# Pair order for the preparations of a seven-product matmul, and residual rows loaded five pairs later

## The chip, the cores and the metric

One core of a Trainium2 chip runs the kernel. Times are microseconds of device time. Three executions of the kernel before were timed; the metric is their median. One further execution was profiled.

## The reference, cut to what matters

One layer of a decoder trunk in float32, 512 tokens of width 2048. Two token mixers (a gated recurrence and a forgetting attention) are projected up, gated and added; the change does not touch them. It touches the two large products that end in a normalised residual:

```python
merged = sigmoid(g_a) * y_a + sigmoid(g_b) * y_b            # 512 x 2048
x = x + rms_norm(merged @ w_o, norm_mix_post)               # w_o: 2048 x 2048
h = rms_norm(x, norm_ffn_pre)
gate, up = split(h @ w_ffn_in, 2)                           # each 512 x 5632
x = x + rms_norm((silu(gate) * up) @ w_ffn_down, norm_ffn_post)   # w_ffn_down: 5632 x 2048
```

## The kernel before, in words

Every float32 operand is cut into a high part (a ScalarE copy to the matmul's fp32r type) and a low part (a VectorE subtraction), and each product is three matmuls: high by low, low by high, high by high. A weight tile of 128 x 1024 thus costs a load on SP's DMA queue into a raw buffer, a copy on ScalarE and a subtraction on VectorE, before TensorE can use it.

`merged @ w_o` and the down projection are done by the class `Rows` as block products of 2 x 2 blocks with seven multiplications in place of eight (p1 to p7). A *pair* is two row blocks of the weights, 2 x 128 rows of 2048 columns, held as four tiles a, b, c, d of 128 x 1024. The products need sums of these tiles, kept in a running tile `t` of the pair, and sums of the activations, written to DRAM beforehand (`md` for `w_o`, `actd` for the down projection; `token_parts`). Since eight PSUM banks hold only two products at a time, the work goes in stages, each of which passes over all pairs: W1 (p7, p6), W2 (p1, p5), W3 (p4), D0 and D1 (p2 and p3, one column half each) over 8 pairs of `w_o`; K1 (p7, p3), K2 (p1, p6), K3 (p5, p2), K4 (p4) over 22 pairs of the down projection. The items of a stage are numbered through: `wo0` to `wo7` are the pairs in W1, `wo8` is the first in W2, `wo24` the first in D0; `dn0` to `dn21` are K1, `dn22` to `dn43` K2, `dn44` to `dn65` K3, `dn66` to `dn87` K4.

For one item, `load` issues on SP's queue the loads of `t` (from the weights in the first stage; of five pairs of the down projection from a DRAM copy later), of the tiles that the stage needs and of the pair's activation sums x (line 749). `split` then issues the copies (lines 771 and 792 on ScalarE), the sums (lines 785 and 816 on VectorE) and the low parts (lines 775 and 825 on VectorE); where `t` lives in DRAM it is written back from SP's queue (line 829). `run` keeps the loads three items and the splits two items ahead of the matmuls in the order in which the program is traced.

That order isn't the order on the engines. The framework's scheduler places the instructions of each engine by readiness in its own timing model, ties going to the earlier traced one; an instruction whose inputs it believes to be there earlier is placed ahead. Once placed, an engine's instructions run strictly in that order, and each waits for its semaphores. `tc.issue_after(ins)` adds, for what its block traces on the same engine as `ins`, the condition that it is placed behind `ins`; nothing waits for `ins` to finish.

Buffers: three raw weight tiles (tag `wraw`, used for a, c, cd, and d in K1), three more (`wrawx`: d in the other stages, and tiles of `t` that live in DRAM), ten part buffers (`wpart`, a high and a low one for each tile in use, four for a pair with two products, two for one with a single product) which TensorE frees, and sixteen tiles of 128 x 1024 (`wide`) which hold most `t`, all x, the norm weights of the last stage and the residual rows.

At the end of a stage the banks are taken (`take`): copies on ScalarE (line 889) or sums on VectorE (lines 883 and 935). When a column block of the output is complete, `done` multiplies it with the norm weights (line 990 for `w_o`, line 1181 for the down projection), and `finish_rows` adds the residual (line 1175) and stores the rows. The residual rows for that are loaded by `x1_hook` in K4 (line 1163), eight loads of 512 KB, one in each of eight successive pairs.

Of the kernel before, what the change touches and what calls it, by code (L numbers as in the profile page):

```python
# [8 lines left out]
F32 = mybir.dt.float32  # L9
F32R = mybir.dt.float32r  # L10
U32 = mybir.dt.uint32
AF = mybir.ActivationFunctionType
ALU = mybir.AluOpType
# [30 lines left out]
def block_kernel(ctx: ExitStack, tc: tile.TileContext, x, w_in, b_fox_f, hgrn_lb_logits, hgrn_norm_w,  # L44
                 w_up_a, w_up_b, w_o, norm_mix_pre, norm_mix_post, norm_ffn_pre, norm_ffn_post,
                 w_ffn_in, w_ffn_down, out):
    nc = tc.nc
# [14 lines left out]
    def wide(name, dtype=F32, shape=(P, 1024)):  # L62
        return bigp.tile(list(shape), dtype, tag="wide", name=name, bufs=NX)
# [54 lines left out]
    loads = []  # L118
    state = {"i": 0}

    def wpart(name):
        return wp.tile([P, 1024], F32R, tag="wpart", name=name, bufs=NHALF)
# [49 lines left out]
    def split(src, name):  # L172

        hi = big(name + "h", F32R)
        lo = big(name + "l", F32R)
        nc.scalar.activation(hi, src, AF.Copy)
        nc.vector.tensor_tensor(lo, src, hi.bitcast(F32), ALU.subtract)
        return hi, lo
# [189 lines left out]
    def hgrn_head(h, r):  # L368
# [99 lines left out]
        for w in range(2):  # L468
            pw = paired(pot, w) if w == 0 else paired(pot, w)[:, :, ::-1]
            ow, gw = [a.rearrange("p (j w t) -> p j w t", w=2, t=P)[:, :, w, :] for a in (o, sg)]  # L470
            nc.vector.scalar_tensor_tensor(ow, pw, nw_f, gw, ALU.mult, ALU.mult)
        oa.append(split(o, n + "o"))
        yield

# [192 lines left out]
    class Rows:  # L667


        def __init__(self, name, w, parts, order, items, done, place_t):  # L670
            self.name, self.w, self.parts, self.order, self.items, self.done = name, w, parts, order, items, done
            self.place_t = place_t
            self.n_loaded = self.n_split = 0
            self.raw, self.ready, self.t, self.acc, self.x_kept, self.later = {}, {}, {}, {}, {}, []

# [9 lines left out]

        def load_to(self, n):
            while self.n_loaded < min(n, len(self.items)):
                self.load(self.n_loaded)
                self.n_loaded += 1

        def load(self, n):
            kind, i = self.items[n]
# [62 lines left out]
        def split_to(self, n):  # L755
            while self.n_split < min(n, len(self.items)):
                self.load_to(self.n_split + 1)
                self.split(self.n_split)
                self.n_split += 1

        def split(self, n):
            kind, i = self.items[n]
            nm = f"{self.name}{n}"
            got = self.raw.pop(n)
            tt = nc.vector.tensor_tensor

            def parts_of(src, tag):

                hi, lo = wpart(f"{nm}{tag}h"), wpart(f"{nm}{tag}l")
                for a, cs in src:  # L770
                    nc.scalar.activation(hi[:, cs], a, AF.Copy)

                def make_lo():
                    for a, cs in src:
                        tt(lo[:, cs], a, hi[:, cs].bitcast(F32), ALU.subtract)
                return hi, lo, make_lo

            def one(which):
                return [(got[which], slice(0, 1024))]

            def add_t(op, a, reverse=False, to=None):

                for u, cs in t:
                    o = u if to is None else to[:, cs]
                    tt(o, *((a[:, cs], u) if reverse else (u, a[:, cs])), op)

            t = one("t") if "t" in got else self.t.get(i)
            names = PRODUCTS[kind]
            width = 256 * len(names)
            xh, xl = got["x"][:, 0:width], got["x"][:, width : 2 * width]  # L790
            if kind != "D1":
                nc.scalar.activation(xh, xl.bitcast(F32), AF.Copy)
            w = {}
            if kind == "K1":
                w["p3"] = parts_of(one("d"), "d")
                add_t(ALU.subtract, got["d"], reverse=True)
                w["p7"] = parts_of(t, "t")
            elif kind == "K2":
                w["p1"] = parts_of(one("a"), "a")
                add_t(ALU.add, got["a"])  # L800
                w["p6"] = parts_of(t, "t")
            elif kind == "K3":
                w["p2"] = parts_of(one("c"), "c")
                add_t(ALU.subtract, got["d"], reverse=True, to=got["d"])
                w["p5"] = parts_of(one("d"), "d")
                if not self.late_c(i):
                    add_t(ALU.subtract, got["c"])
            elif kind in ("K4", "W3"):
                if "c" in got:
                    add_t(ALU.subtract, got["c"])  # L810
                w["p4"] = parts_of(t, "t")
            elif kind == "W1":
                add_t(ALU.subtract, got["d"], reverse=True, to=got["d"])
                w["p7"] = parts_of(one("d"), "d")
                for u, cs in t:
                    tt(u, got["a"][:, cs], got["d"][:, cs], ALU.add)
                w["p6"] = parts_of(t, "t")
            elif kind == "W2":
                w["p1"] = parts_of(one("a"), "a")
                add_t(ALU.subtract, got["d"], reverse=True, to=got["d"])  # L820
                w["p5"] = parts_of(one("d"), "d")
            else:
                w["cd"] = parts_of(one("cd"), "c")
            if kind != "D1":
                tt(xl, xl.bitcast(F32), xh.bitcast(F32), ALU.subtract)
            for v in w.values():
                v[2]()
            if "t" in got and kind in ("K1", "K2") or "t" in got and kind == "K3" and not self.late_c(i):
                nc.sync.dma_start(self.t[i], got["t"])
            if kind[0] == "D":  # L830
                q = int(kind[1])
                h, l, _ = w["cd"]
                wq = {("p2", q): (h[:, F], l[:, F]), ("p3", q): (h[:, L], l[:, L])}
            else:
                wq = {(p, q): (w[p][0][:, (F, L)[q]], w[p][1][:, (F, L)[q]]) for p in names for q in range(2)}
            self.ready[n] = (wq, {p: (xh[:, j * 256 : (j + 1) * 256], xl[:, j * 256 : (j + 1) * 256])
                                  for j, p in enumerate(names)})
# [262 lines left out]
    def parts_to(i):  # L1100
        while ahead["w"] < min(i, len(work)):
            n = ahead["w"]
            ahead["w"] += 1
            j, p, _ = work[n]
            key = key_of(n)
            load_to(n + 1)
            a, b, c, d = (raws.get(key + (x,)) for x in "abcd")
            if p == "p7":
                nc.vector.tensor_tensor(d, d, b, ALU.subtract)  # L1109
            elif p == "p5":  # L1110
                nc.vector.tensor_tensor(b, b, a, ALU.subtract)
            elif p == "p6":
                nc.vector.tensor_tensor(a, a, d, ALU.add)  # L1113
            elif p == "p4":
                nc.vector.tensor_tensor(c, a, c, ALU.subtract)
            src = {"p1": a, "p2": c, "p3": d, "p7": d, "p5": b, "p6": a, "p4": c}[p]
            wh = wpart(f"fh{n}")
            wl = wpart(f"fl{n}")
            nc.scalar.activation(wh, src, AF.Copy)  # L1119
            nc.vector.tensor_tensor(wl, src, wh.bitcast(F32), ALU.subtract)  # L1120
            wparts[n] = (wh, wl)
# [14 lines left out]
    def ffn_ahead():  # L1136
        load_to(4)
        parts_to(2)
# [17 lines left out]
                wfp.extend((r[:, 0:S], r[:, S : 2 * S]))  # L1156

    def x1_hook(at):
        if 1 <= at < 9:
            t, half = t_row((at - 1) // 2), (at - 1) % 2  # L1160
            with tc.issue_after(loads[-1].ins):
                r = wide(f"x1r{t}_{half}")
                nc.sync.dma_start(r, x1d[t * P : (t + 1) * P, half * 1024 : (half + 1) * 1024])
                x1r[t, 2 * half], x1r[t, 2 * half + 1] = r[:, 0:S], r[:, S : 2 * S]
        if at in (10, 12):
            finish_rows(2 + (at - 10) // 2)

    def t_row(t):
        return (t + 2) % 4
# [3 lines left out]
    def finish_rows(t):  # L1173
        for c in range(4):
            nc.vector.scalar_tensor_tensor(mw[t, c], mw[t, c], rinv[t], x1r[t, c], ALU.mult, ALU.add)
            nc.sync.dma_start(out[t * P : (t + 1) * P, c * S : (c + 1) * S], mw[t, c])
# [18 lines left out]
    gt, ut, tt, prod, open_bank, acts = {}, {}, {}, {}, {}, {}  # L1195
    for n, (j, p, place) in enumerate(work):
        load_to(n + LOAD_AHEAD)
        parts_to(n + AHEAD)
        for i in range(2 * (n - 4), 2 * (n - 3)):
# [3 lines left out]
        at = place.index(p)  # L1203
# [3 lines left out]
        for i in range(KH):  # L1207
            cs = slice(i * P, (i + 1) * P)
# [71 lines left out]
```

## Time and profile before

| what | value |
|---|---|
| median of three executions | 2837.89 us (2835.57 to 2845.24) |
| the profiled execution | 2837.45 us |
| its span, first to last instruction | 2835.7 us |
| TensorE busy | 2766.2 us |
| VectorE busy | 1931.0 us |
| ScalarE busy | 1170.1 us |
| mean granted TensorE clock, as a share of full | 0.993 |

The seven-product stages stand at 1292 to 1468 us (`w_o`) and at 2371 to 2824 us (down projection) of the span. A row of a timeline is: start, duration, engine and line, operation, written tile <- read tiles, shapes, count; behind it in brackets the idle time of the engine just before and what ended it. PE is TensorE, DVE VectorE, ACT ScalarE, POOL GpSimd; SPq is SP's queue, which only issues transfers. Tile names carry the item's number; `dh`, `dl` are the high and low part of tile d, `th`, `tl` of t; buffer numbers are left out, so `dnt` and `wot` are the t of any pair. In a table by stretch the columns are: from and to, its length, busy us and number of instructions of PE, PEld (weight loads of TensorE), DVE, ACT and POOL, mean granted clock, mean busy share of the DMA engines, GB/s.

### The profile page before, as it was taken

To read this page: it belongs to the slowest core of one execution; us is meant where nothing else is said; L and a number is where in the kernel's file an instruction comes from. 1 tells how busy PE (TensorE), PEld (TensorE's weight loads), DVE (VectorE), ACT (ScalarE), POOL (GpSimd) and SP (SyncE) were. 2 spreads that over 40 slices of the span, in tenths; PEclk is the share of its full clock that TensorE was granted. 3 is DMA by queue.
4 is the path that set the end of the run, shared out by engine and by line. 5 is a ranking of instruction groups with operands and counts; after the bars stand their busy time and mean duration, and the time that the engine had idled before them with its cause. 6 is when DMAs were issued, how large, how long until landed. Compare 5 with 4: busy or idle time off the path is not lost.

```text
span 2835.7 us, 40418 instructions
## 1 busy us (share of the span) xinstructions
PE 2766.2 (98%) x16024; PEld 2433.8 (86%) x16024; DVE 1931.0 (68%) x2750; ACT 1170.1 (41%) x1557; POOL 45.0 (2%) x75
## 2 busy tenths in 40 slices
PE   9999999999999999998999999999999999999997
PEld 7788888888888888887789999999999999877876
DVE  4776675333343433457879988888888888777888
ACT  4554544222232342224565444444444444444444
POOL 1000000000000000000000000000000000000001
PEclk9999999999999999999999999999999999999999
DMA  6323323333333333467774544444444448755875
GB/s 164 97 75 85 82 76 85 97 97 97 101 90 89 89 86 99 128 209 255 241 233 117 178 144 123 127 131 129 126 124 132 128 127 267 246 171 172 279 260 175
DMA packets 504799, 406.39 MB, mean 143 GB/s; under 512 B 16617, under 2 KB 444186, under 8 KB 504610
## 3 DMA queue, kind: packets, MB, share of 16 engines
q1 hardware_dynamic: 504610, 403.81, 47.6%
q8 instruction: 126, 2.06, 0.3%
q14 instruction: 63, 0.52, 0.1%
HBM read 359.95 MB, written 43.79 MB: 142 GB/s over the span
## 4 chain that ended last, share of the span: by engine, by line
PE 84%; DMA 6%; DVE 6%; issue 2%; ACT 2%; SPq 0%; POOL 0%; DVEq 0%; POOLq 0%; ACTq 0%
PE b L152 3%; PE b L154 3%; PE b L153 3%; PE p L152 3%; PE p L153 3%; PE p L154 3%; PE ga L152 2%; PE ga L153 2%; PE ga L154 2%; PE gb L152 2%; PE gb L153 2%; PE gb L154 2%; PE ya L152 1%; PE ya L154 1%; PE ya L153 1%
## 5 line engine op out<-in xcount | busy, mean ns | idle before, releaser
L136 ACT ACTIVATE wh<-wr 128x1024 fp32r<-128x1024 f32 (+1 forms) x214 | 223.0, 1043 | 642.4 <-PE b L153 147.0
L137 DVE TENSOR_TENSOR wl<-wr,wh 128x1024 fp32r<-128x1024 f32 (+1 forms) x214 | 257.9, 1205 | 232.7 <-ACT wh L136 232.6
L1119 ACT ACTIVATE fh<-fid 128x1024 fp32r<-128x1024 f32 x88 | 93.3, 1060 | 182.5 <-DVE fid L1109 119.1
L152 PE MATMUL p<-x,wh 128*128 128x512 f32 x416 | 165.2, 397 | 1.7 <-DVE rb L272 1.7
L154 PE MATMUL p<-x,wl 128*128 128x512 f32 x416 | 164.6, 396 | 0.0
L153 PE MATMUL p<-x,wh 128*128 128x512 f32 x416 | 163.5, 393 | 0.0
L152 PE MATMUL b<-x,wh 128*128 128x512 f32 x384 | 154.1, 401 | 0.0
L154 PE MATMUL b<-x,wl 128*128 128x512 f32 x384 | 150.2, 391 | 0.0
L153 PE MATMUL b<-x,wh 128*128 128x512 f32 x384 | 149.7, 390 | 0.0
L1120 DVE TENSOR_TENSOR fl<-fic,fh 128x1024 fp32r<-128x1024 f32 x88 | 107.5, 1222 | 40.4 <-ACT fh L1119 38.4
L1119 ACT ACTIVATE fh<-fia 128x1024 fp32r<-128x1024 f32 x88 | 93.2, 1059 | 96.7 <-DVE fia L1113 18.3
L1119 ACT ACTIVATE fh<-fic 128x1024 fp32r<-128x1024 f32 x88 | 93.2, 1059 | 72.0 <-issue 44.6
L1120 DVE TENSOR_TENSOR fl<-fid,fh 128x1024 fp32r<-128x1024 f32 x88 | 107.6, 1223 | 21.7 <-ACT fh L1119 21.6
L1120 DVE TENSOR_TENSOR fl<-fia,fh 128x1024 fp32r<-128x1024 f32 x88 | 107.3, 1220 | 15.9 <-ACT fh L1119 15.9
L152 PE MATMUL gb<-x,wh 128*128 128x512 f32 x256 | 100.7, 393 | 0.9 <-ACT wh L136 0.9
L152 PE MATMUL ga<-x,wh 128*128 128x512 f32 x256 | 100.5, 392 | 0.0
L154 PE MATMUL ga<-x,wl 128*128 128x512 f32 x256 | 100.1, 391 | 0.0
L154 PE MATMUL gb<-x,wl 128*128 128x512 f32 x256 | 99.8, 390 | 0.0
L153 PE MATMUL ga<-x,wh 128*128 128x512 f32 x256 | 99.7, 390 | 0.0
L153 PE MATMUL gb<-x,wh 128*128 128x512 f32 x256 | 99.6, 389 | 0.0
L152 PEld LDWEIGHTS p<-x,wh 128*128 128x128 f32 x416 | 78.3, 188 | 16.4 <-DVE rb L272 1.9
L154 PEld LDWEIGHTS p<-x,wl 128*128 128x128 f32 x416 | 78.3, 188 | 15.2
(5943 smaller groups left out, 8800.8 us busy)
## 6 DMA issues: line engine op xcount, KB each, us to landing
wr<-in_w_in_dram SPq DMA_DIRECT2D x166, 512.0 KB, 3.9
fic<-in_w_ffn_in_dram SPq DMA_DIRECT2D x52, 512.0 KB, 4.3
fia<-in_w_ffn_in_dram SPq DMA_DIRECT2D x52, 512.0 KB, 5.1
fid<-in_w_ffn_in_dram SPq DMA_DIRECT2D x44, 512.0 KB, 4.0
fib<-in_w_ffn_in_dram SPq DMA_DIRECT2D x44, 512.0 KB, 3.9
wr<-in_w_up_a_dram SPq DMA_DIRECT2D x16, 512.0 KB, 3.9
wr<-in_w_up_b_dram SPq DMA_DIRECT2D x16, 512.0 KB, 3.9
actd<-g SPq DMA_DIRECT2D x22, 256.0 KB, 2.4
```

Of the source, the lines that this page charges most:

```text
L136: hi = nc.scalar.activation(wh[:, 0:width], raw[:, 0:width], AF.Copy)
L137: lo = nc.vector.tensor_tensor(wl[:, 0:width], raw[:, 0:width], wh[:, 0:width].bitcast(F32), ALU.subtract)
L152: nc.tensor.matmul(ps, lhsT=wh, rhs=xl, start=first, stop=False)
L153: nc.tensor.matmul(ps, lhsT=wh, rhs=xh, start=False, stop=False)
L154: nc.tensor.matmul(ps, lhsT=wl, rhs=xh, start=False, stop=last)
L1119: nc.scalar.activation(wh, src, AF.Copy)
L1120: nc.vector.tensor_tensor(wl, src, wh.bitcast(F32), ALU.subtract)
```

## The change

The items' copies, sums and low parts, and loads, are placed behind those of the item before: `self.last` keeps the last copy (`hi`), the last low part (`lo`) and the last load (the x load) of the item before, and `behind` opens `issue_after` blocks for them. ScalarE's instructions of `split` are then placed behind the last copy of the item before, VectorE's behind its last low part, and the loads of `load` behind its x load. The residual rows are loaded at hooks 6 to 13 of K4 in place of 1 to 8, and rows 2 and 3 are finished at hooks 12 and 14 in place of 10 and 12.

```diff
@@ class Rows, __init__
+            self.last = {}
@@ class Rows
         def load_to(self, n):
             while self.n_loaded < min(n, len(self.items)):
-                self.load(self.n_loaded)
+                with self.behind("load"):
+                    self.load(self.n_loaded)
+                self.last["load"] = loads[-1]
                 self.n_loaded += 1
+
+        def behind(self, *keys):
+
+            stack = ExitStack()
+            for key in keys:
+                if key in self.last:
+                    stack.enter_context(tc.issue_after(self.last[key].ins))
+            return stack
@@ split_to
-                self.split(self.n_split)
+                with self.behind("hi", "lo"):
+                    self.split(self.n_split)
@@ split
+            last = {}
...
-                    nc.scalar.activation(hi[:, cs], a, AF.Copy)
+                    last["hi"] = nc.scalar.activation(hi[:, cs], a, AF.Copy)
...
-                        tt(lo[:, cs], a, hi[:, cs].bitcast(F32), ALU.subtract)
+                        last["lo"] = tt(lo[:, cs], a, hi[:, cs].bitcast(F32), ALU.subtract)
...
             for v in w.values():
                 v[2]()
+            self.last.update(last)
@@ x1_hook
-        if 1 <= at < 9:
-            t, half = t_row((at - 1) // 2), (at - 1) % 2
+        if 6 <= at < 14:
+            t, half = t_row((at - 6) // 2), (at - 6) % 2
...
-        if at in (10, 12):
-            finish_rows(2 + (at - 10) // 2)
+        if at in (12, 14):
+            finish_rows(2 + (at - 12) // 2)
```

## Rows read from the trace of the kernel before

**Rows 1.** The page, section 1: busy time, share of the span, instructions.

```profile
PE 2766.2 (98%) x16024; PEld 2433.8 (86%) x16024; DVE 1931.0 (68%) x2750; ACT 1170.1 (41%) x1557; POOL 45.0 (2%) x75
```

**Rows 2.** Busy time by stretch, core 0: W1's start, W1, W2, W3, D0, K1 to K4.

```profile
1284.00:1292.00 8.00, 0.20 (x2) 0.15 (x1) 5.12 (x8) 2.31 (x3) 0.00 (x0) 0.67 0.87 268
1292.00:1333.00 41.00, 41.00 (x171) 33.71 (x172) 32.36 (x36) 17.88 (x22) 0.00 (x0) 0.94 0.78 255
1333.00:1381.00 48.00, 48.00 (x213) 39.57 (x212) 37.23 (x38) 23.50 (x34) 0.00 (x0) 1.00 0.87 283
1381.00:1410.00 29.00, 26.44 (x114) 20.81 (x114) 28.61 (x44) 18.46 (x34) 0.00 (x0) 1.00 0.64 199
1410.00:1438.00 28.00, 21.48 (x81) 16.28 (x80) 19.21 (x31) 13.78 (x28) 3.35 (x4) 0.88 0.82 255
2371.00:2494.00 123.00, 120.79 (x528) 98.41 (x526) 91.87 (x110) 54.65 (x72) 0.00 (x0) 1.00 0.74 250
2494.00:2624.60 130.60, 122.93 (x529) 98.31 (x529) 95.68 (x107) 62.50 (x85) 0.00 (x0) 1.00 0.55 178
2624.60:2749.70 125.10, 121.27 (x530) 98.56 (x528) 105.63 (x117) 53.08 (x63) 0.00 (x0) 1.00 0.81 274
2749.70:2792.00 42.30, 32.43 (x122) 25.34 (x122) 39.31 (x64) 24.05 (x51) 8.60 (x2) 0.88 0.68 229
```

**Rows 3.** Waits of TensorE: waiter and line, releaser, total us, times, longest.

```profile
PE woW1p L158 <- DVE sgb L516: 7.8, 1, 7.8
...
PE woD0p L159 <- DVE wo25cl L775: 4.4, 1, 4.4
```

**Rows 4.** Timeline of VectorE and ScalarE, in K1.

```profile
2450.46 1.22 DVE L785 TENSOR_TENSOR dnt<-dn17d,dnt 128x1024 f32<-128x1024 f32 x1 [3.20 <-DMA dn17d<-in_w_ffn_down_dram]
2451.61 1.22 DVE L775 TENSOR_TENSOR dn15dl<-dn15d,dn15dh 128x1024 fp32r<-128x1024 f32 x1
2451.64 1.04 ACT L771 ACTIVATE dn16dh<-dn16d 128x1024 fp32r<-128x1024 f32 x1
...
2457.70 1.23 DVE L785 TENSOR_TENSOR dn18t<-dn18d,dn18t 128x1024 f32<-128x1024 f32 x1 [3.14 <-DMA dn18d<-in_w_ffn_down_dram]
2458.84 1.22 DVE L775 TENSOR_TENSOR dn16dl<-dn16d,dn16dh 128x1024 fp32r<-128x1024 f32 x1
```

**Rows 5.** Timeline of SP's queue, in K1.

```profile
2452.85 0.33 SPq L703 DMA_DIRECT2D dn18d<-in_w_ffn_down_dram  x1
...
2460.09 0.33 SPq L703 DMA_DIRECT2D dn19d<-in_w_ffn_down_dram  x1
```

**Rows 6.** Timeline of SP's queue, head of K4.

```profile
2762.67 0.38 SPq L1163 DMA_DIRECT2D x1r<-x1d  x1
2765.15 0.32 SPq L749 DMA_DIRECT2D dn71x<-actd  x1
```

**Rows 7.** Timeline of all engines, from the merge into W1.

```profile
1284.12 0.33 SPq L703 DMA_DIRECT2D wo4d<-in_w_o_dram  x1
...
1289.91 1.23 DVE L785 TENSOR_TENSOR wo4d<-wo4d,wot 128x1024 f32<-128x1024 f32 x1 [2.88 <-DMA wo4d<-in_w_o_dram]
1291.05 0.68 DVE L516 TENSOR_TENSOR sgb<-yb,sgb 128x512 f32<-128x512 f32 x1
```

**Rows 8.** Timeline of VectorE and TensorE, from K3 into K4.

```profile
2749.65 1.23 DVE L785 TENSOR_TENSOR dnt<-dnt,dn73c 128x1024 f32<-128x1024 f32 x1 [1.01 <-DMA dn73c<-in_w_ffn_down_dram]
...
2753.47 0.68 DVE L883 TENSOR_TENSOR dn00c<-dnK3p,dn00c 128x512 f32<-128x512 f32 x1
...
2754.30 0.68 PE L158 MATMUL dnK4p<-dn66th,dn66x 128*128 128x512 f32 x1 [4.43 <-ACT dn68x L792]
...
2759.45 1.27 DVE L883 TENSOR_TENSOR dn11c<-dnK3p,dn11c 128x512 f32<-128x512 f32 x2
```

**Rows 9.** Timeline of VectorE, in W2: the first and last sum for W3.

```profile
1364.08 1.23 DVE L785 TENSOR_TENSOR wot<-wot,wo16c 128x1024 f32<-128x1024 f32 x1 [0.56 <-DMA wo16c<-in_w_o_dram]
...
1379.50 1.22 DVE L785 TENSOR_TENSOR wot<-wot,wo21c 128x1024 f32<-128x1024 f32 x1
```

## The prediction, made before the changed kernel was run

> **What bounds the kernel now.** The page comes first: of the span of 2835.7 us TensorE is busy for 2766.2, 98% [rows 1]. So nothing but idle or slowed TensorE time can be won. The change touches only the seven-product stages (W1 to W3, D0 and D1 for `w_o`, K1 to K4 for the down projection), so the second view is the table of busy times by stretch, for these stages alone [rows 2]. The reader is to see in it that W2 has no idle time: 213 matmuls in 48.00 us, 0.2254 us each, so a pair of weight rows with 24 matmuls (W1, W2, K1 to K3) costs TensorE 5.41 us and one with 12 (W3, K4) 2.70 us. At this rate every other stretch is too long:
>
> - start of W1 (8.00 us, 2 matmuls): 8.0 lost; W1's own stretch: 41.0 - 171 x 0.2254 = 2.5
> - W3: 29.0 - 25.7 = 3.3; the head of D0: 28.0 - 18.3 = 9.7
> - K1: 123.0 - 119.0 = 4.0; K2: 130.6 - 119.2 = 11.4; K3: 125.1 - 119.5 = 5.6, together 21.0
> - K4's head: 42.3 - 27.5 = 14.8
>
> That is 59.3 us in all, the most that a better order could win. Busy times show less than this (K2: 122.93 of 130.60), since a matmul's record overlaps the next one's; so I count matmuls.
>
> The third view, the waits, names VectorE or what it feeds: the first W1 matmul waits 7.8 us for an eviction (`sgb`), one of D0 4.4 us for a low part [rows 3]. The fourth, the timeline of VectorE in K1, shows why [rows 4]. At 2450.46 stands the sum of pair 17, after 3.20 us of waiting for that pair's load; the low parts of pair 15, which TensorE wants next, start behind it. The same again at 2457.70: 3.14 us for load 18, and only then pair 16's low part. SP's queue closes the loop [rows 5]: load 18 is issued at 2452.85, as pair 15's low part ends and frees its raw buffer, and load 19 only at 2460.09, after pair 16's. So low part, load (some 4.8 us, 2452.85 to 2457.70), sum, low part run in series, 7.2 us in this turn against TensorE's 5.41. It is order, not amount: in K2 VectorE is busy 95.68 of 130.60 us.
>
> **The change, part by part.** It adds no instruction, only issue order: a pair's copies on ScalarE, its sums and low parts on VectorE and its loads on SP stand behind the last ones of the pair before. VectorE's steps on a whole tile are 1.22 us long and 1.14 start to start (2457.70, 2458.84 [rows 4]); on half a tile 0.6 start to start (ten evictions from 2753.47 to 2759.45 [rows 8]).
>
> K1 to K3. In pair order a sum no longer stands before an older pair's low part. A pair needs three or four whole steps and a half one, 4.0 to 5.2 us, under 5.41: VectorE keeps up. A raw buffer (three of them) then has three pairs, 16.2 us, for transfer 4.8, copy 1.04 on ScalarE [rows 4], x part 0.6, sum 1.14, low part 1.14: 8.7 us. The 21.0 us should go. What is late next is the change of stage, where eight banks are emptied. What it will cost no row shows; it lies between nothing and the 4.6 us at K4's start now (2749.7 to 2754.3, below). Nearest is W1 to W2, a change without idle time at its end [rows 2]. I keep 5.0 for the three changes together: **-16.0**, ends -20 and, three times 4.6 kept, -7.
>
> Start of W1. Load `wo4d` is issued at 1284.12, VectorE stands before its sum until 1289.91, and the eviction that TensorE needs follows at 1291.05 [rows 7]. With the change pair 4's sums come after pair 3's low parts, which need part buffers that W1 itself has to free; so that sum can't stand there. The eviction follows the last matmul by its own 0.7 us and perhaps one step of 1.2: 2.0 us stay of 8.0. W1's own 2.5 us belong to it: the granted clock has a mean of 0.67 over the 8 idle us and 0.94 in the stretch after them, so part of both ran at the lower level (1.2 GHz of 2.4), while W2, without idle time, has 1.00 [rows 2]. So I let the slow clock go with the idle time: **-8.5**, ends -10 and -2. The Trainium skill has it as a rule (TensorE: Matmul & The Clock Gate, "What's actually happening"): the throttled state is the default and activity lifts it. The rows agree; were the clock independent of idle time, this term would be -6.0.
>
> W2 to D0. Here the change takes something away. VectorE makes six sums for W3 ahead, the first at 1364.08, the last at 1379.50 [rows 9], in W2, where it is busy 37.23 of 48.00 us; in W3 it is busy 28.61 of 29.00 [rows 2]. In pair order a sum may go only as far ahead as the part buffers let the low parts go: ten, two for a W3 pair, so up to five pairs. If none of them can be made ahead, 6 x 1.14 = 6.8 us fall on the path in W3; if whole pairs are done ahead in their stead, nothing. Then W3 and D0 stay bound by VectorE's same amount of work. I take **0**, nearer to the row for W2, which has 10.8 us of VectorE idle; ends +6.8 and -5 (half of D0's 9.7; its 4.4 us wait [rows 3] is for a low part of pair 25, behind row updates that stay where they are).
>
> K3 to K4. After K3's last low parts VectorE makes sums for pairs up to 75 (2749.65 stands after 1.01 us of waiting for a load) before the first eviction at 2753.47; TensorE, whose K4 banks these evictions free, has nothing from 2749.7 until 2754.30, 0.15 us after the first of them ends. (The row names a copy of x68 as what ended the wait; pair 66 doesn't read it.) From 2753.47 on VectorE has 12 evictions and 12 products with the norm weights on tiles of the same size, 24 x 0.6 = 14.4 us, and pair 69's low part behind them [rows 8]. In pair order the sums of 69 to 75 are behind, evictions start as banks fill, and TensorE enters K4 with up to four pairs ready, 10.8 us. It needs pair 70 by then, and VectorE has 14.4 us less what it emptied before, some 1.8, plus 1.5 for the pair: 3.3 us short; with the first bank's 0.7 and a rest, I keep 4.8 of 14.8: **-10.0**, ends -14 and 0.
>
> The later residual rows (eight 512 KB loads). At 2762.67 such a load stands in SP's queue before x71, issued 2765.15 [rows 6]; both take `wide` buffers. Five pairs later more of these are free. Alone I take it at nothing, since VectorE's products cover it there; without that cover x71 is late by the 2.5 us between the two issues. The cost: row 2's four updates are made at the twelfth hook, six pairs (16 us) after its first load, and the last load is nine pairs, 24 us, before the end. Both exceed the transfer; if the queue holds them, up to 2 us at the end.
>
> New waits. VectorE's low part two pairs ahead waits for a part buffer that TensorE frees; behind it stand evictions and later sums. ScalarE's copies wait for the same buffers, behind them the next x part. On SP a load waits behind the previous pair's x load, which waits for a `wide` buffer; behind it weight loads and the write-backs of t. All are at least a pair ahead of need as long as the lead of two pairs is kept.
>
> The sum: 8.5 + 0 + 16.0 + 10.0 = 34.5 us. The profiled execution took 2837.45 us (span 2835.7 and 1.75 around it), 0.44 below the median of the three runs, 2837.89; I make no correction for that. 2837.45 - 34.5 = 2803.0.
>
> **The rivals.** *Too few buffers.* The gaps in K1 to K3 repeat, and load 18 is issued just as a raw buffer comes free [rows 5]. If three raw buffers are the limit whatever the order, the 21.0 us stay and only the starts of W1 and K4 gain: 2837.45 - 18.5 = 2819. The Trainium skill reads repeating gaps so (Perfetto Trace Analysis, "Optimization Strategy": consistent bubbles can mean that there is not enough memory for the next tile). Against it stands that the buffer is held by a low part that itself waits behind a sum. Chance 0.17.
>
> *Head of line moved to the part buffers (slower).* In pair order VectorE stands before a low part whose buffer TensorE has not freed, and does later what it does now in that time: 14 sums made ahead (six for W3, four each for W1 and K4), 14 x 1.14 = 16.0 us, into stretches where it is nearly always busy (28.61 of 29.00; 39.31 of 42.30 in K4's head). If its waits for buffers replace its waits for loads in K1 to K3 and the eviction before W1 stands behind one pair's remaining steps, so that 2.3 us are won there, the time is 2837.45 + 16.0 - 2.3 = 2851. It decides where VectorE's chain from a freed buffer to the low part exceeds the pair and a half of lead, 8.1 us. By the steps above it is some 5 us. Chance 0.08.
>
> *Nothing to speak of.* The scheduler may place the evictions and the x parts as unluckily as before, or the order may hold already: 2837. For it: in W1 and W2 most loads are in pair order now. Against it: [rows 4] and [rows 7]. Chance 0.09.
>
> **How the numbers follow.** Forecast 0.66, too few buffers 0.17, nothing 0.09, slower 0.08. A difference of 0.3%, 8.5 us, is about what a measurement here can tell from no change. The forecast's ends reach from 2837.45 - 49 = 2788 to about 2826; leaving a tenth off each side and taking in 2819, the range is 2791 to 2829. Faster by over 0.3%: 0.66 + 0.17 = 0.83.
>
> **What would show it.** Right: on VectorE in K1 a sum never before an older pair's low part, and no wait of 3 us for a load in front of one; K2 near 120 us; the first W1 matmul within 3 us of the last of the merge; K4's first within 1 us of K3's last. W3 and D0 as long as now. Wrong: VectorE idle before low parts with a matmul as the releaser while TensorE waits for the same pair; W3 longer by some 7 us; SP standing before x loads.

## The result, and the profile after

| | before | after |
|---|---|---|
| median of four executions each | 2836.73 us (2834.99 to 2845.24) | 2809.41 us (2807.72 to 2810.74) |
| ratio, with its 95% interval | | 0.9897 [0.9876, 0.9919] |
| the profiled execution, and its span | 2837.45 us, 2835.7 | 2810.27 us, 2808.6 |

Faster by 27.3 us, 1.0%. The page after, its head and section 1 (span; busy time, share, instructions):

```profile
span 2808.6 us, 40502 instructions
PE 2758.4 (98%) x16024; PEld 2433.5 (87%) x16024; DVE 1930.5 (69%) x2750; ACT 1170.8 (42%) x1557; POOL 40.7 (1%) x75
```

The same instructions stand there as in [rows 1], and VectorE and ScalarE are as busy as before. Only the order changed. The table of busy times by stretch, after (columns as in [rows 2]): W1's start, W1, W2, W3, D0, K1, K2, K3, K4.

```profile
1284.00:1286.00 2.00, 0.38 (x3) 0.04 (x1) 1.97 (x4) 1.72 (x2) 0.00 (x0) 1.00 0.95 320
1286.00:1329.60 43.60, 43.60 (x192) 36.10 (x193) 39.10 (x41) 22.12 (x30) 0.00 (x0) 1.00 0.86 288
1329.60:1373.10 43.50, 43.50 (x193) 36.02 (x193) 33.67 (x37) 22.12 (x31) 0.00 (x0) 1.00 0.89 285
1373.10:1401.60 28.50, 24.70 (x97) 18.65 (x97) 25.93 (x35) 12.36 (x22) 0.00 (x0) 0.94 0.51 161
1401.60:1436.80 35.20, 26.33 (x98) 19.76 (x97) 25.84 (x43) 19.21 (x39) 4.42 (x4) 0.85 0.80 244
2368.50:2488.40 119.90, 119.87 (x530) 98.98 (x529) 98.52 (x119) 61.50 (x82) 0.00 (x0) 1.00 0.76 260
2488.40:2608.10 119.70, 119.70 (x530) 99.15 (x529) 92.28 (x104) 59.82 (x79) 0.00 (x0) 1.00 0.61 202
2608.10:2727.80 119.70, 119.70 (x530) 99.15 (x529) 108.71 (x123) 55.43 (x67) 0.00 (x0) 1.00 0.78 265
2727.80:2796.10 68.30, 62.59 (x266) 49.91 (x264) 61.34 (x96) 34.33 (x71) 2.78 (x2) 0.98 0.68 227
```

W1, W2 and K1 to K3 have next to no idle time left: busy time equals length (K1: all but 0.03 us), with 0.226 us for a matmul. W3, D0 and K4 still have it. The waits of TensorE name the places (four rows of the list; the others in these stages are at most 1.9 us):

```profile
PE woD0p L158 <- ACT mo L1016: 5.7, 1, 5.7
PE dnK4p L158 <- DVE rs_v L194: 5.4, 1, 5.4
...
PE woW3p L158 <- DVE wo20x L838: 2.5, 1, 2.5
...
PE woW1p L158 <- DVE sgb L516: 1.6, 1, 1.6
```

The wait for `sgb` before W1 fell from 7.8 us [rows 3] to 1.6, and the waits for low parts in K1 to K3 are gone. In D0 and K4 a first wait of over 5 us stands. The engines named there (`mo` on ScalarE, `rs_v` on VectorE) are only the instructions that ended last before it by the profile; which steps TensorE really waited for is read below from the timelines.

Where the 27.2 us of the two spans' difference come from follows from the starts of TensorE's matmuls in the two timelines (last matmul of one stage, first of the next), in us:

| place | before | after | change | predicted |
|---|---|---|---|---|
| last merge matmul to first of W1 | 8.2 | 2.0 | -6.2 | |
| half-clock matmuls at W1's start | 2.4 | 0.0 | -2.4 | together -8.5 |
| W2's end, wait of W3's first matmul for a bank | 2.0 | 0.2 | -1.8 | |
| W3 and D0, first matmul to first of D1 | 55.2 | 63.7 | +8.5 | with the row above 0 |
| first of K1 to last of K3 | 378.7 | 359.1 | -19.6 | -16.0 |
| K3's last to K4's first, and K4 | 74.8 | 68.3 | -6.4 | -10.0 |
| all else (D1 to K1, both ends) | | | +0.7 | |
| sum | | | -27.2 | -34.5 |

Now the mechanism. VectorE in K1, after:

```profile
2439.18 1.22 DVE L798 TENSOR_TENSOR dnt<-dn15d,dnt 128x1024 f32<-128x1024 f32 x1
2440.31 0.69 DVE L838 TENSOR_TENSOR dn15x<-dn15x 128x512 fp32r<-128x512 f32 x1
2442.34 1.23 DVE L788 TENSOR_TENSOR dn15dl<-dn15d,dn15dh 128x1024 fp32r<-128x1024 f32 x1 [1.34 <-PE dnK1p L159]
2443.48 1.22 DVE L788 TENSOR_TENSOR dn15tl<-dnt,dn15th 128x1024 fp32r<-128x1024 f32 x1
2444.62 1.29 DVE L798 TENSOR_TENSOR dnt<-dn16d,dnt 128x512 f32<-128x512 f32 x2
```

SP's queue in K1, after:

```profile
2438.15 0.33 SPq L714 DMA_DIRECT2D dn17d<-in_w_ffn_down_dram  x1
...
2443.59 0.33 SPq L714 DMA_DIRECT2D dn18d<-in_w_ffn_down_dram  x1
...
2449.03 0.33 SPq L714 DMA_DIRECT2D dn19d<-in_w_ffn_down_dram  x1
```

Pair 15's sum, x part and low parts now stand together, and pair 16's sum behind them; no sum waits for its load here. The loads follow each other by 5.44 us, TensorE's time for a pair, where it was 7.24 in [rows 5]. VectorE does wait, 1.34 us before a low part whose buffer TensorE has just freed. This costs nothing: that low part is done by 2443.6, and TensorE's first matmul of pair 15 comes, without a wait, at 2450.46.

### The profile page after: what moved, and what is told of

Its sections match the earlier page's. It is cut to its first block, busy times and chain, and to the rows that moved or that the text cites. A ratio compares the mean times of both kernels' runs of the same rounds, so it can differ in the third digit from the quotient of the medians.

```text
span 2808.6 us, 40502 instructions
## 1 busy us (share of the span) xinstructions
PE 2758.4 (98%) x16024; PEld 2433.5 (87%) x16024; DVE 1930.5 (69%) x2750; ACT 1170.8 (42%) x1557; POOL 40.7 (1%) x75
## 4 chain that ended last, share of the span: by engine, by line
PE 91%; DVE 4%; ACT 2%; DMA 1%; issue 1%; POOL 0%; SPq 0%; DVEq 0%; POOLq 0%; ACTq 0%
PE b L152 3%; PE b L154 3%; PE b L153 3%; PE p L152 3%; PE p L153 3%; PE p L154 3%; PE gb L152 2%; PE ga L154 2%; PE ga L153 2%; PE gb L153 2%; PE gb L154 2%; PE ga L152 2%; PE dnK1p L158 1%; PE dnK1p L159 1%; PE dnK2p L159 1%; PE dnK2p L158 1%
```

## The experiments

The intervals are those of the ratio to the kernel before, run beside each. Stage lengths are from the matmul starts of one profiled execution, from a stage's first to the next one's first (K4: first to last).

**E1 and E2: which order does it.** E1 keeps VectorE's order alone, E2 that of the loads alone (the residual rows stay late in both).

```diff
 E1
-                with self.behind("load"):
-                    self.load(self.n_loaded)
+                self.load(self.n_loaded)
-                with self.behind("hi", "lo"):
+                with self.behind("lo"):
                     self.split(self.n_split)
 E2
-                with self.behind("hi", "lo"):
-                    self.split(self.n_split)
+                self.split(self.n_split)
```

> Of the three orders only VectorE's is kept (sums, x parts and low parts behind the last low part of the pair before); copies and loads are placed freely again. Theory (VectorE's order is the cause): K1 to K3 take 359 to 363 us from the first K1 matmul to the first of K4 (384 before, 359 with the change), the gap ahead of W1 is 2 to 3 us (8.2 before), total 2806 to 2813. Rival (the loads' order on SP is the cause): K1 to K3 take 375 to 384 us and the total is 2825 to 2837.

> Only the loads are kept in pair order; ScalarE and VectorE are placed freely; the residual rows stay five pairs later. Theory: nothing is won in K1 to K3 (380 to 386 us) and the gap ahead of W1 stays 7 to 9 us; total 2831 to 2839. Rival (loads): K1 to K3 360 to 370 us, total 2808 to 2820.

E1: 2815.38 us, 0.992 [0.9905, 0.9935]; E2: 2837.86 us, 0.9999 [0.999, 1.0008]. VectorE's order alone has some 22 of the 27 us, though its total misses the 2806 to 2813 that I expected; its other two numbers, 362.5 us for K1 to K3 and a gap of 2.0 us before W1, came as forecast. The loads' order alone has nothing in the total. That zero is a sum: from K1's first matmul to K4's first it takes 378.6 us (383.5 before), and K4 takes 74.9 (69.9 before). In E2 the timeline of VectorE in K1 has the old picture, sum first and waiting:

```profile
2452.12 1.22 DVE L797 TENSOR_TENSOR dnt<-dn17d,dnt 128x1024 f32<-128x1024 f32 x1 [2.92 <-DMA dn17d<-in_w_ffn_down_dram]
2453.26 1.22 DVE L787 TENSOR_TENSOR dn15dl<-dn15d,dn15dh 128x1024 fp32r<-128x1024 f32 x1
```

What E1 lacks beside the changed kernel lies at K3 and K4. Its waits of TensorE there:

```profile
PE dnK4p L158 <- DVE rs_v L194: 7.2, 1, 7.2
...
PE dnK4p L158 <- DVE dn00c L896: 2.4, 1, 2.4
```

**E11: is it the loads' order or ScalarE's?** All but the loads' order (`behind("load")` taken out as in E1, ScalarE's order kept).

> The changed kernel without the order of the loads (copies and low parts kept in pair order). E1 lacked the order of loads and of copies and lost 6 us to the change, in K3 (122.6 us against 119.7) and K4 (72.4 against 68.1). Theory (x and weight loads out of pair order are what is late there): as E1, total 2813 to 2817, K4 71 us or more. Rival (the copies' order on ScalarE is what E1 lacked): K3 119.5 to 120.5, K4 68 to 69, total 2808 to 2811.

2814.96 us, 0.9912 [0.9896, 0.9929]: E1's time, with K4 at 73.7 us and K3 at 123.9 against 68.1 and 119.7. So by the medians the loads' order is worth some 5 us, but only on top of VectorE's; the intervals of E11 and of the changed kernel overlap. ScalarE's order, added to VectorE's, shows no gain; by itself it was not run.

**E3 and E10: the residual rows.** E3 is the changed kernel with the rows loaded at hooks 1 to 8 again and finished at 10 and 12; E10 is the kernel before with only the later rows.

```diff
 E3, on the changed kernel (E10 is the reverse, on the kernel before)
-        if 6 <= at < 14:
-            t, half = t_row((at - 6) // 2), (at - 6) % 2
+        if 1 <= at < 9:
+            t, half = t_row((at - 1) // 2), (at - 1) % 2
...
-        if at in (12, 14):
-            finish_rows(2 + (at - 12) // 2)
+        if at in (10, 12):
+            finish_rows(2 + (at - 10) // 2)
```

> The changed kernel with the residual rows loaded at the old hooks (1 to 8, finished at 10 and 12). Theory (this part is worth nothing by itself, VectorE's products cover it): K4 67 to 70 us from first to last matmul (68.1 with the change), total 2808 to 2812. Rival (in pair order an x load held by residual rows holds everything behind it): K4 72 us or more, total 2813 to 2820.

> The kernel before with nothing but the later residual rows (hooks 6 to 13, finished at 12 and 14). Theory (they matter only where pair order holds other work behind an x load; in the old order VectorE's products cover them): total 2834 to 2840, K4 69 to 72 us (69.9 before). Rival (worth 3 to 4 us in either order, as E3 showed in the new one): total 2831 to 2834, K4 66 us or less.

E10: 2837.48 us, 0.9997 [0.9988, 1.0007]: nothing in the old order. E3: 2812.74 us, 0.9908 [0.989, 0.9926], with K4 at 72.1 us against 68.1. E3's K4 lies where the rival had it, its total between the two ranges. By the medians the part is worth some 3 us in pair order, but the intervals of E3 and of the changed kernel overlap; K4's length in programs with the same K4 (68.1, 69.9 and 68.5 us in the changed kernel, E4 and E5) scatters by 1.7, less than the 4.0 between these two. In E3 SP's queue at K4's head has row loads among the x loads, and ScalarE waits for pair 73's x:

```profile
2745.61 0.32 SPq L1177 DMA_DIRECT2D x1r<-x1d  x1
2746.03 0.38 SPq L760 DMA_DIRECT2D dn73x<-actd  x1
...
2751.99 0.42 ACT L805 ACTIVATE dn73x<-dn73x 128x256 fp32r<-128x256 f32 x1 [3.50 <-DMA dn73x<-actd]
```

One matmul of K4 then waits 1.3 us for pair 73's low part, which the changed kernel's K4 does not show; there x73 is issued at 2736.25, ahead of the row loads.

**E4 and E5: what W3 lost.** In the changed kernel VectorE's timeline shows this in the last three of W3's eight pairs (and for the first two, prepared in W2):

```profile
1392.52 1.22 DVE L798 TENSOR_TENSOR wot<-wot,wo22c 128x1024 f32<-128x1024 f32 x1
1393.65 0.42 DVE L838 TENSOR_TENSOR wo22x<-wo22x 128x256 fp32r<-128x256 f32 x1
1394.92 1.22 DVE L788 TENSOR_TENSOR wo22tl<-wot,wo22th 128x1024 fp32r<-128x1024 f32 x1 [0.85 <-ACT wo22th L784]
1396.07 1.22 DVE L798 TENSOR_TENSOR wot<-wot,wo23c 128x1024 f32<-128x1024 f32 x1
```

A pair's one tile is t. So its sum, its copy on ScalarE (1.06 us) and its low part run in series, and with no other pair's sum allowed between them VectorE stands idle 0.85 us in such a pair: 3.55 us a pair (1392.52 to 1396.07) against TensorE's 2.7. E4 frees W3 from the order. E5 keeps it, but lets the sums of a W3 pair go ahead of the low part of the one pair before, and no further.

```diff
 E4
-                with self.behind("hi", "lo"):
+                keys = () if self.items[self.n_split][0] == "W3" else ("hi", "lo")
+                with self.behind(*keys):
 E5
+                w3 = self.items[self.n_split][0] == "W3"
+                before = self.last.get("lo")
-                with self.behind("hi", "lo"):
+                with self.behind("hi", "lo_before" if w3 else "lo"):
                     self.split(self.n_split)
+                self.last["lo_before"] = before
 E5, in split: x's low part and the low parts of the tiles
+            with self.behind("lo"):
...
```

> The changed kernel, but W3's pairs are split without the new order on ScalarE and VectorE. Theory (in W3 the order costs time, since a next pair's sum may no longer fill the wait for a copy or be made in W2): W3 and D0 together 54 to 58 us from the first W3 matmul to the first of D1 (55.2 before, 63.7 with the change), total 2801 to 2805. Rival (the loss there comes from where evictions and row updates stand, not from W3's own pairs): 62 to 65 us and 2808 to 2811.

> The changed kernel; in W3 alone a pair's sum may stand behind the last low part of two pairs before, so one pair ahead and no more. Theory (copy latency: in pair order VectorE stands 0.85 us in each W3 pair, since sum, copy and low part follow each other and no other pair's sum may fill the wait): the waits of 0.85 us are gone and W3 takes 24 to 26 us from its first matmul to the first of D0 (28.5 with the change, 24.6 with W3 free). Rival (the six sums that were made in W2): one pair ahead is too little, W3 stays at 27.5 to 29 us.

E4: 2805.74 us, 0.9885 [0.9869, 0.99], W3 24.6 us in place of 28.5. W3 and D0 together take 58.9 us, and this and the total lie just outside the ranges of both the theory and the rival, since D0 stays long. E5: 2803.38 us, 0.988 [0.9865, 0.9895], W3 24.2; all its executions lie below all of the changed kernel's, though the intervals overlap. VectorE in E5:

```profile
1387.60 1.22 DVE L801 TENSOR_TENSOR wot<-wot,wo22c 128x1024 f32<-128x1024 f32 x1
1388.74 1.21 DVE L791 TENSOR_TENSOR wo21tl<-wot,wo21th 128x1024 fp32r<-128x1024 f32 x1
1389.87 0.41 DVE L842 TENSOR_TENSOR wo22x<-wo22x 128x256 fp32r<-128x256 f32 x1
1390.21 1.21 DVE L791 TENSOR_TENSOR wo22tl<-wot,wo22th 128x1024 fp32r<-128x1024 f32 x1
```

Pair 22's sum fills the time of pair 21's copy, and the wait is gone there. One pair of freedom does as well as no order at all, so the six sums need not be made as far ahead as the old order made them. But the waits are only half of what W3 lost. The busy times of W3 alone (columns as in [rows 2]), before, after and in E5:

```profile
1383.30:1406.80 23.50, 22.58 (x97) 17.95 (x98) 23.50 (x34) 14.75 (x25) 0.00 (x0) 1.00 0.58 178
1373.20:1401.70 28.50, 24.70 (x98) 18.65 (x97) 25.93 (x35) 12.46 (x22) 0.00 (x0) 0.94 0.51 161
1373.30:1397.40 24.10, 22.63 (x97) 17.68 (x96) 23.25 (x33) 11.40 (x20) 0.00 (x0) 1.00 0.52 162
```

VectorE (the third busy time) sets W3's pace in all three: it has no idle time there but the waits for a copy. Of the 5.0 us from 23.5 to 28.5, it is idle for 2.6 (three waits) and busy for 2.4 more. By W3's first matmul the old order had made nine of the stage's sixteen sums and low parts, pair order five, E5 seven: in the changed kernel pair 18's low part (1375.39) and pair 19's sum (1377.12) fell behind the evictions of W2's banks, which E5 has before them (1368.91, 1367.77). TensorE's longest wait in W3, 2.5 us for pair 20's x part, stands behind these.

**E6 and E9: K4's wait.** In the changed kernel VectorE emptied the banks, did all twelve products with the norm weights and only then pair 69's sum (from 2739.76), x part and low part. TensorE's first matmul of the pair, which reads the x part and the copy made from the sum, waited 5.4 us:

```profile
2732.47 0.68 DVE L1195 TENSOR_TENSOR mw<-dn00c,wfp 128x512 f32<-128x512 f32 x1
...
2738.48 1.28 DVE L1195 TENSOR_TENSOR mw<-dn11c,wfp 128x512 f32<-128x512 f32 x2
...
2741.08 0.41 DVE L838 TENSOR_TENSOR dn69x<-dn69x 128x256 fp32r<-128x256 f32 x1
...
2741.64 0.77 PE L158 MATMUL dnK4p<-dn69th,dn69x 128*128 128x512 f32 x1 [5.42 <-DVE rs_v L194]
```

This wait is not new. Before the change it stood at the same pair, behind the same twelve products:

```profile
PE dnK4p L158 <- DVE rs_v L194: 4.9, 1, 4.9
```

E6 (on E4) lets go two of these products per pair, each behind the last low part. E9 has E5's looser order in K4 too, with E6 and E7.

```diff
 E6
-                while n > n0 and self.later:
-                    self.later.pop(0)()
+                for _ in range(2 if kind == "K4" else len(self.later)):
+                    if n > n0 and self.later:
+                        with self.behind(*(("lo",) if kind == "K4" else ())):
+                            self.later.pop(0)()
 E9, on E5, E6 and E7
-                w3 = self.items[self.n_split][0] == "W3"
+                w3 = self.items[self.n_split][0] in ("W3", "K4")
```

> The kernel with W3 free (E4), and in K4 the twelve products with the norm weights are traced two per pair and placed behind the low parts traced so far. Theory (the 5.8 us wait for pair 69 at K4's head is these products standing in front of its low part): no wait over 2 us in K4, K4 62 to 65 us from first to last matmul (69.9 in E4), total 2799 to 2802. Rival (VectorE's amount of work is the limit): the wait moves to a later pair, K4 67 us or more, total as E4.

> E5 extended and joined with E6 and E7: sums may go one pair ahead in W3 and in K4, K4's products with the norm weights are spread two per pair behind the low parts, D0's first two pairs are split before W3's banks are taken. Theory (in K4, too, VectorE's chain of sum, copy and low part leaves waits that another pair's sum can fill): K4 61 to 65 us from first to last matmul (67.2 in E8, 68.1 with the change), total 2794 to 2800. Rival (VectorE's work in K4's head is the limit by its amount): K4 66 us or more, total 2800 to 2804.

E6: 2803.79 us, 0.988 [0.9865, 0.9894]. The wait on pair 69 is gone, but K4 is 68.3 us against 69.9 in E4; the 62 to 65 that I expected were missed. The waits of TensorE in E6 say why:

```profile
PE dnK4p L158 <- ACT dn73th L785: 1.3, 1, 1.3
PE dnK4p L159 <- DVE dn81tl L789: 1.1, 1, 1.1
```

The long wait has broken into short ones, pairs later. E9 was to remove these with the freedom that helped W3: 2805.16 us, 0.9883 [0.9868, 0.9897], K4 71.0 us. It did not; new waits stand before x parts of pairs 83 and 84 (1.2 and 1.1 us). The rival written down before E9, that VectorE's amount of work is the limit, is not ruled out: its range for K4 (66 us or more) was met, its total passed by 1.2 us, and VectorE is busy 61.3 us of the changed kernel's K4, more than the 60 us that 264 matmuls at 0.226 take. What K4 would need stays open.

**E7 and E8: D0's wait.** D0's first wait is for pair 25, whose x part and low part stand behind the row updates after W3 (in the changed kernel VectorE begins the x part at 1409.45, and TensorE's first matmul of the pair comes at 1410.28). E7 (on E4) prepares two pairs more before W3's banks are taken; E8 is E6 and E7 together.

```diff
 E7
-            self.split_to(n1)
+            self.split_to(n1 + (2 if kind == "W3" else 0))
```

> The kernel with W3 free (E4), and the first two pairs of D0 are split before W3's banks are taken. Theory (the wait of 5.9 us at D0's second pair is its low part standing behind W3's evictions and row updates): that wait is gone, D0 27 to 30 us (34.3 in E4), total 2799 to 2803. Rival (D0 is bound by the row updates and late loads behind them): the wait moves to the next pairs, D0 32 us or more, total as E4 within 2 us.

> E6 and E7 together in one kernel: if both theories hold, the total is 2793 to 2799 us; if only one of them does, 2799 to 2803.

E7: 2805.78 us, 0.9886 [0.987, 0.9903], D0 31.8 us, where 27 to 30 was expected: missed. E8: 2802.64 us (2798.03 to 2804.18), 0.9874 [0.9859, 0.9889], D0 32.2. E8's total lies in the range written for one theory holding, but neither K4 (67.2 us) nor D0 came into the ranges of E6 and E7. Pair 25 is now ready in time, but TensorE waits 3.5 us for pair 26, behind the same row updates, and later for pairs 30 and 31 (0.5 and 2.0 us), whose loads are late. SP's queue in E8:

```profile
1406.93 0.80 SPq L748 DMA_DIRECT2D wo29cd<-in_w_o_dram  x2
1410.59 2.31 SPq L1018 DMA_DIRECT2D x1d<-xr  x4
1412.99 0.91 SPq L748 DMA_DIRECT2D wo30cd<-in_w_o_dram  x2
1413.95 1.85 SPq L1002 DMA_DIRECT2D xr<-in_x_dram  x4
1415.89 1.19 SPq L748 DMA_DIRECT2D wo31cd<-in_w_o_dram  x2
```

and ScalarE in E8:

```profile
1419.15 1.06 ACT L785 ACTIVATE wo30ch<-wo30cd 128x1024 fp32r<-128x1024 f32 x1 [4.38 <-DMA wo30cd<-in_w_o_dram]
...
1424.70 1.06 ACT L785 ACTIVATE wo31ch<-wo31cd 128x1024 fp32r<-128x1024 f32 x1 [3.96 <-DMA wo31cd<-in_w_o_dram]
```

Pair 30's load is issued behind four stores of updated rows, pair 31's behind four loads of residual rows, and both pairs' copies wait some 4 us for their loads. That the stores and row loads hold them is read from the order of issue, not tested; whether another queue for these would free D0 was not tried.

E8 has the lowest median, with all its executions below all of the changed kernel's. Against E5 and E6 its lead of about 1 us is within their spread.

## Why the prediction was right, and where its steps were not

The sign, the size (27 us of 34.5 forecast) and the main cause held: in K1 to K3 and before W1 it was the order on VectorE, not the amount of its work or the number of buffers. Two sums of the prediction are off without touching this: W1's start lost some 7.5 us and not 8.0 (two matmuls stand in those 8.00 us), and the terms' upper ends (-7, -2, +6.8, 0) give 2835, not "about 2826".

**W1's start**, -8.5: measured -6.2 and -2.4, the sum as forecast. The eviction now stands right behind the last merge matmul, with one step before it; the timeline of VectorE and TensorE after:

```profile
1284.03 1.22 DVE L829 TENSOR_TENSOR wot<-wo2a,wo2d 128x1024 f32<-128x1024 f32 x1
...
1285.17 0.68 DVE L516 TENSOR_TENSOR sgb<-yb,sgb 128x512 f32<-128x512 f32 x1
...
1285.99 0.47 PE L158 MATMUL woW1p<-wo0dh,wo0x 128*128 128x512 f32 x1 [1.62 <-DVE sgb L516]
```

The slow clock did go with the idle time: granted 0.67 and 0.94 in [rows 2], 1.00 in both stretches now.

**K1 to K3**, -16.0: measured -19.6. The mechanism was right and the term mis-sized: the 5.0 us kept for the changes of stage were too many. All three stages run at 119.7 to 120.0 us, so the changes cost next to nothing.

**W2 to D0**, "I take 0": this is the step that failed. It measured +6.7 (8.5 less 1.8), near its upper end of +6.8, and only in part for that end's reason. The 0 needed "whole pairs ... done ahead in their stead" and "VectorE's same amount of work" in W3; but five steps were done ahead in place of nine, and VectorE had 25.9 us of work in W3 in place of 23.5. I had left out what stands between a sum and its low part. In a stage with two products other steps of the same pair stand in the copy's time; with one product only the short x part does, and pair order forbids the next pair's sum. The waits for the copy held the chain back in W2 (two of 0.85 us) and left VectorE idle for 2.6 us in W3. E4 and E5 show it: W3 from 28.5 to 24.6 and 24.2 us. Of the +6.7, W3 has 5.1 less the 1.8 won at W2's end, and D0 3.5. D0's share isn't settled: it took 30.7 to 34.3 us in E4 to E9, and 34.3 and 30.7 of these in E4 and E6, which differ in K4 alone.

**K3 to K4**, -10.0: measured -6.4. The entry went as forecast: TensorE's gap between the stages is 0.2 us, from 4.8. The failing step is "with up to four pairs ready, 10.8 us": only pairs 66 to 68 were ready, 8.1 us, and the twelve products stood before pair 69's steps (2732.47 to 2739.76). So TensorE waited 5.4 us where 3.3 had been put, and slow matmuls followed (below). E6 shows that the rest of K4 has little slack: with that wait removed, others took its place. So what was won here is the entry (4.6 us) and 1.8 us of slowed or idle time in K4; the wait for pair 69, 4.9 us before, was not shortened.

**The residual rows**, "Alone I take it at nothing": right as put (E10). In pair order, where a late x load holds all loads behind it, the profile of E3 gives the part about 4 us of K4.

**The rivals.** *Too few buffers* fell: the same three raw buffers, and K2 at 119.7 us. The Trainium skill (Perfetto Trace Analysis, "Optimization Strategy") reads consistent bubbles as possibly too little memory for the next tile; here the trace disagrees, since they came from a sum placed before an older pair's low part, and went without any more memory. *Head of line moved to the part buffers* has its wait (about 1.3 us in most pairs of K1), but VectorE's chain stays inside the lead, as the prediction had it. Of the sums it priced as returning to the later stages, W3 shows a part (2.4 us more work there); the rest of W3's loss is idle time at the copy.

## What to carry to other kernels

When an in-order engine prepares tiles for another, look for a step on newer data placed before an older tile's last step: a repeated wait there can be an order and not a shortage, and forcing the order of that one engine is the first thing to try. Before an order is made strict, count the hand-overs to another engine inside one tile's chain: where a tile has only one chain, letting one step of the next tile in can pay, as in W3; in K4, which has evictions and products too, it did not. Gains at several places need their own bounds by stage: here three places won 35 us and one gave 7 back.

## What the runs showed that was not expected

- A strict order cost 0.85 us on VectorE for the copy on ScalarE in five of W3's eight pairs, and one pair of freedom removed all but one of these waits; the same freedom in K4, beside evictions and products, did not help (E9, 71.0 us).
- TensorE's clock. After the waits of 5 to 6 us in D0 and K4 the matmuls run 0.43 us start to start in place of 0.23, and the granted mean of D0's stretch is 0.85. In W3, after a wait of 2.5 us (and one of 1.1 just before), they run 0.43 apart from 1389.71 to 1392.27, and the granted mean of the stage is 0.94. After the 2.0 us gap before W1 the second step is 0.23 already, with the granted clock at 1.00. So a wait can cost more than its length. The Trainium skill (TensorE: Matmul & The Clock Gate, "What's actually happening") has activity lift a throttled clock; the rows agree.
- The order of the loads was worth nothing alone (E2, 0.9999) and some 5 us on top of VectorE's order (the changed kernel beside E11): an order that acts only on top of another. By the intervals, which overlap, the 5 us are not certain.
